# Eight split weight buffers of a decoder trunk, each beginning at its own 64-byte step modulo 512

## The chip, the cores and the metric

The kernel runs as one program on one core of a Trainium2 chip. The time is the device time of one execution in microseconds (us); a lower number is better. Times of the kernel before come from two runs, and the profile from one profiled execution.

## The reference, cut to what matters

The reference computes a decoder trunk of two layers over 512 tokens of width 1024 in float32. Every layer sends the normalised residual stream through one input projection, whose columns feed three groups of heads (latent attention, a pooling mixer and a matrix memory), through one output projection, and through a gated feed-forward part of inner width 2816:

```python
def reference(x, ...):
    h = layer_norm(x, ln0_g, ln0_b)
    for l in range(DEPTH):
        proj = h @ w_in[l]
        cq, ckv, kr, xp, xqk, xv, xo, ipre, fpre = jnp.split(proj, _split_points(), axis=-1)
        a = mla(cq, ckv, kr, g_qn[l], w_uq[l], g_kvn[l], w_ukv[l], cos, sin)
        p = multiscale_pool(xp, w_pool[l], s_pool[l])
        m = mlstm(xqk, xv, xo, ipre, fpre, ...)
        mix = jnp.concatenate([a, p, m], axis=-1) @ w_out[l]
        h = layer_norm(ALPHA * h + mix, ln1_g[l], ln1_b[l])
        f = conv_glu_ffn(h, w_up[l], w_fconv[l], b_fconv[l], w_down[l])
        h = layer_norm(ALPHA * h + f, ln2_g[l], ln2_b[l])
    return h
```

All weight products are dense float32 products; the two largest are `h @ w_up` (1024 by 5632) and `... @ w_down` (2816 by 1024).

## The kernel before, in words

**Split products.** Each float32 operand x is split into hi, which is x cast to the format float32r, and lo = x - hi, cast as well. A product is then three matmuls that add into the same PSUM bank: hi times hi, hi times lo, lo times hi. `mm3` (L159 to L162) does this with the weights as the stationary operand, and `tm_gemm` (L284 to L286) does it with the weights as the moving operand. In a call `T.matmul(o, a, b)` the operand `a` is stationary: a LDWEIGHTS instruction loads its 128 columns, which are 512 bytes in each partition, and there is one LDWEIGHTS for each matmul. The operand `b` is moving and streams through, mostly 512 columns, which are 2048 bytes in each partition. The LDWEIGHTS of a matmul runs while the matmul before it streams.

**Weights.** All weights stand in one list in the order of their use, 93 pieces for each layer and 186 in all, each 128 partitions by up to 1024 floats. `fetch` (L139 to L147) takes the next piece: a DMA from SP's queue into one of two `raw` buffers, the cast into a `hi` buffer on ScalarE (L145), and the subtraction into a `lo` buffer (L146) on VectorE, or on GpSimd for some pieces. There are four hi and four lo buffers, taken in turn, so that piece n reuses the buffers of piece n - 4. `getw` calls `fetch` one piece ahead of the use.

**Stages of a layer.** The input projection is done in pieces `ia` (456 columns at a time), `it` and `ib`; then come the up-projections of attention `uq`, `uk` and `uv`, attention (`s` is scores, `pt` transposed probabilities, `o` values), the output projection (tile name `o` as well, with `hi_o` and `lo_o` as its weights), the feed-forward's up part (`t_up`, 44 pieces for each layer) and its down part (`d`, 22 pieces for each layer). The normalised stream lies transposed in `a_hi` and `a_lo`, the feed-forward's inner activations in `f_hi` and `f_lo`.

**Order.** TensorE's order is written by a small planner (`Order`), which merges instruction streams by fixed costs and due times; the other engines keep program order under a scheduler. Neither reads an address.

**Where the buffers lie.** A tile pool lays its buffers one after the other in SBUF. Each `hi` or `lo` buffer of 1024 floats takes 4096 bytes in a partition, a whole multiple of 512. The start of each buffer in a partition, modulo 512, in the built program:

| buffers | before |
|---|---|
| all four hi and all four lo | 320 |
| a_hi, a_lo (blocks of 512 bytes) | 320 |
| f_hi, f_lo (blocks of 512 bytes) | 128 |
| cq_hi, cq_lo, ck_hi, ck_lo | 0 |
| pt_hi, pt_lo | 0 |
| v (values, four tiles) | 128, 0, 384, 128 |
| qn (queries, four heads) / kn (keys, four heads) | 0, 128, 256, 384 / 256, 256, 384, 256 |

In the up part and in `it` the moving operand is a block of `a_hi` or `a_lo`, and the weights are stationary; in `ia`, `ib` and the output projection it is the other way round. In `d` a weight buffer moves and a block of `f_hi` or `f_lo` is stationary. In `uq` and `uk` the weights are stationary against moving `cq` or `ck`; in `uv` the weights move and `ck` is stationary. In attention `pt` moves against stationary `v`, and `kn` against stationary `qn`.

Of the kernel before, what the change touches and what calls it, by code (L numbers as in the profile page):

```python
# [11 lines left out]
F32R = mybir.dt.float32r  # L12
# [6 lines left out]
P = 128  # L19
# [22 lines left out]
CH = 1024  # L42
# [7 lines left out]


class Order:
    """Merges instruction streams into one order for the tensor engine."""

    def __init__(self):
        self.now = 0.0
# [37 lines left out]
def trunk(ctx: ExitStack, tc: tile.TileContext, I: dict, out: bass.AP, layers=DEPTH):  # L94
# [5 lines left out]
    stream = ctx.enter_context(tc.tile_pool(name="stream", bufs=3))  # L100
# [28 lines left out]
    def bank(name):  # L129
        return psum.tile([P, S], F32, tag="ps", name=name)  # L130

# [1 line left out]
    wlist = []  # L133
    wloaded = []

# [3 lines left out]
    def fetch():  # L139
        src, n, name, eng = wlist[len(wloaded)]  # L140
        raw = stream.tile([P, CH], F32, tag="raw", bufs=2, name="raw_" + name)[:, :n]
        nc.sync.dma_start(raw, src)
        hi = stream.tile([P, CH], F32R, tag="whi", bufs=4, name="hi_" + name)
        lo = stream.tile([P, CH], F32R, tag="wlo", bufs=4, name="lo_" + name)
        A.copy(hi[:, :n], raw)  # L145
        eng.tensor_tensor(lo[:, :n], raw, hi[:, :n].bitcast(F32), ALU.subtract)  # L146
        wloaded.append((hi, lo, name))  # L147
# [3 lines left out]
    def getw(name, ahead=1):  # L151
        while len(wloaded) <= min(used[0] + ahead, len(wlist) - 1):
            fetch()
        hi, lo, nm = wloaded[used[0]]
        assert nm == name, (nm, name)
        used[0] += 1
        return hi, lo
# [206 lines left out]
            for q in range(NF // 2):  # L364
                add_w(I["w_dn"][l, half, q], 1024, f"d{l}_{half}_{q}", V)

# [1 line left out]
    ln0 = ExitStack()  # L368
    lp = ln0.enter_context(tc.tile_pool(name="ln0", bufs=1))
    h = lp.tile([P, NT, D], F32, name="h0")  # L370
# [5 lines left out]
    for i in range(NT):  # L376
        for a in range(0, D, D // 2 if i == 0 else D):
            n = D // 2 if i == 0 else D
            nc.sync.dma_start(h[:, i, a : a + n], I["x"][i * P : (i + 1) * P, a : a + n])
        if i == 0:  # L380
            cols0 = lp.tile([P, 2 * KD], F32, name="cols0")
            nc.sync.dma_start(cols0, I["ln0_c"])
        if i < 3:
            fetch()
        if i == 0:
            nc.sync.dma_start(ident, I["ident"])
# [643 lines left out]
```

## Time and profile before

| | us |
|---|---|
| median of 2 runs (1220.02 to 1220.42) | 1220.22 |
| profiled execution, first to last instruction (its span) | 1215.6 |
| median less span | 4.6 |
| TensorE (PE) busy with matmuls | 1169.8 |
| PE busy with weight loads (PEld) | 954.2 |
| VectorE (DVE) / ScalarE (ACT) / GpSimd (POOL) busy | 640.7 / 474.3 / 282.3 |

The profiled execution's own time is known by its span only; the 4.6 us between the span and the median of the other runs are taken as work around the span that this change doesn't touch. A duration of a matmul in the profile is a modelled one: a matmul's row ends later than the next one starts, so how fast matmuls follow each other is read from the distance of their starts.

### The profile page before, as it was taken

What the parts mean: (1) busy time and instruction counts of PE and PEld (TensorE: products, weight loads), DVE (VectorE), ACT (ScalarE), POOL (GpSimd) and SP (SyncE); (2) the same over time, 40 slices, a digit from 0 to 9 for tenths busy, and PEclk for the clock granted to TensorE, in tenths of its full rate; (3) what the DMA queues carried; (4) which work ended last, traced back from release to release, by engine and by line L of the source; (5) the groups of instructions that cost most, each with busy time, mean ns of one, the idle gap of its engine ahead of it and who ended that gap; (6) DMA issues with size and microseconds to landing.
All of it is one profiled execution on the core that took longest, in us unless ns stands there. A gap on an engine that the chain in (4) does not pass through costs nothing.

```text
span 1215.6 us, 14103 instructions
## 1 busy us (share of the span) xinstructions
PE 1169.8 (96%) x5426; PEld 954.2 (79%) x5426; DVE 640.7 (53%) x929; ACT 474.3 (39%) x815; POOL 282.3 (23%) x240
## 2 busy tenths in 40 slices
PE   5999999989999999999999999997999999999996
PEld 3877878878888888888887787786888888888884
DVE  7775785665434434223388559648544343432325
ACT  4654453525333333211257535525433333331210
POOL 4315610272111111000123264006311111110003
PEclk8999999989999999999999999999999999999998
DMA  5531214123233232323234103041332323322221
GB/s 197 204 118 48 77 53 156 54 102 123 93 98 104 87 104 89 102 87 104 64 137 151 63 31 104 12 180 52 138 101 91 104 88 103 97 94 93 98 70 69
DMA packets 34786, 119.71 MB, mean 98 GB/s; under 512 B 4376, under 2 KB 4888, under 8 KB 34720
## 3 DMA queue, kind: packets, MB, share of 16 engines
q1 hardware_dynamic: 34432, 118.30, 29.2%
q8 instruction: 42, 0.69, 0.2%
q10 hardware_dynamic: 288, 0.52, 0.1%
q14 instruction: 24, 0.20, 0.0%
HBM read 112.50 MB, written 6.31 MB: 98 GB/s over the span
## 4 chain that ended last, share of the span: by engine, by line
PE 77%; DVE 11%; POOL 5%; ACT 3%; issue 2%; DMA 1%; SPq 0%; POOLq 0%; DVEq 0%; ACTq 0%
PE t_up L161 13%; PE t_up L162 13%; PE t_up L160 13%; PE d L286 6%; PE d L284 6%; PE d L285 6%; PE o L284 2%; PE o L285 2%; PE o L286 2%; DVE a_lo L166 1%; POOL ps L521 1%; POOL py L525 1%; PE ib L284 1%; DVE qp L715 1%; PE ib L285 1%
## 5 line engine op out<-in xcount | busy, mean ns | idle before, releaser
L160 PE MATMUL t_up<-a_hi,hi_up 128*128 128x512 f32 (+1 forms) x752 | 284.7, 379 | 9.1 <-ACT a_hi L165 9.1
L161 PE MATMUL t_up<-a_lo,hi_up 128*128 128x512 f32 (+1 forms) x752 | 285.1, 379 | 2.4 <-DVE a_lo L166 2.4
L162 PE MATMUL t_up<-a_hi,lo_up 128*128 128x512 f32 (+1 forms) x752 | 284.1, 378 | 0.0
L146 DVE TENSOR_TENSOR lo_up<-raw_up,hi_up 128x1024 fp32r<-128x1024 f32 x86 | 115.1, 1338 | 172.7 <-ACT hi_up L145 169.2
L160 PEld LDWEIGHTS t_up<-a_hi,hi_up 128*128 128x128 f32 x752 | 143.5, 191 | 34.7 <-ACT a_hi L165 9.5
L145 ACT CAST hi_up<-raw_up 128x1024 fp32r<-128x1024 f32 x88 | 92.8, 1055 | 191.1 <-PE t_up L161 168.0
L161 PEld LDWEIGHTS t_up<-a_lo,hi_up 128*128 128x128 f32 x752 | 143.3, 191 | 29.2 <-DVE a_lo L166 3.1
L905 POOL TENSOR_TENSOR f_lo<-y,f_hi 128x512 fp32r<-128x512 f32 x44 | 77.2, 1753 | 376.1 <-ACT f_hi L904 376.1
L162 PEld LDWEIGHTS t_up<-a_hi,lo_up 128*128 128x128 f32 x752 | 143.5, 191 | 25.7
L146 DVE TENSOR_TENSOR lo_d<-raw_d,hi_d 128x1024 fp32r<-128x1024 f32 x44 | 53.8, 1224 | 165.1 <-ACT hi_d L145 164.7
L284 PE MATMUL d<-hi_d,f_hi 128*128 128x512 f32 x352 | 139.4, 396 | 0.0
L286 PE MATMUL d<-hi_d,f_lo 128*128 128x512 f32 x352 | 139.2, 396 | 0.0
L285 PE MATMUL d<-lo_d,f_hi 128*128 128x512 f32 x352 | 139.2, 395 | 0.0
L145 ACT CAST hi_d<-raw_d 128x1024 fp32r<-128x1024 f32 x44 | 46.3, 1052 | 182.0 <-PE d L286 163.0
L286 PEld LDWEIGHTS d<-hi_d,f_lo 128*128 128x128 f32 x352 | 66.2, 188 | 15.9
L284 PEld LDWEIGHTS d<-hi_d,f_hi 128*128 128x128 f32 x352 | 66.2, 188 | 15.9
L285 PEld LDWEIGHTS d<-lo_d,f_hi 128*128 128x128 f32 x352 | 66.2, 188 | 15.8
L903 DVE TENSOR_TENSOR y<-y,t_up 128x512 f32<-128x512 f32 x44 | 30.2, 687 | 78.1 <-PE t_up L162 74.8
L898 DVE SCALAR_TENSOR_TENSOR y<-t_up,pp,y 128x511 f32<-128x511 f32 x88 | 65.6, 746 | 1.6
L899 ACT ACTIVATE y<-y 128x512 f32<-128x512 f32 x44 | 27.8, 632 | 90.2 <-DVE y L898 90.2
L284 PE MATMUL o<-hi_o,a_hi 128*128 128x512 f32 x128 | 50.9, 398 | 0.0
L286 PE MATMUL o<-hi_o,a_lo 128*128 128x512 f32 x128 | 50.0, 390 | 0.0
(263 smaller groups left out, 1924.0 us busy)
## 6 DMA issues: line engine op xcount, KB each, us to landing
raw_up<-in_w_up_dram SPq DMA_DIRECT2D x88, 512.0 KB, 3.5
raw_d<-in_w_dn_dram SPq DMA_DIRECT2D x44, 512.0 KB, 3.5
raw_o<-in_w_out_dram SPq DMA_DIRECT2D x16, 512.0 KB, 3.5
raw_it<-in_w_it_dram SPq DMA_DIRECT2D x12, 512.0 KB, 3.7
spill<-h SPq DMA_DIRECT2D x8, 512.0 KB, 2.8
raw_ib<-in_w_ib_dram SPq DMA_DIRECT2D x8, 512.0 KB, 3.5
h<-spill SPq DMA_DIRECT2D x8, 512.0 KB, 5.1
raw_ia<-in_w_ia_dram SPq DMA_DIRECT2D x8, 456.0 KB, 4.6
```

Of the source, the lines that this page charges most:

```text
L145: A.copy(hi[:, :n], raw)
L146: eng.tensor_tensor(lo[:, :n], raw, hi[:, :n].bitcast(F32), ALU.subtract)
L160: T.matmul(o, whi, xhi, start=start, stop=False)
L161: T.matmul(o, whi, xlo, start=False, stop=False)
L162: T.matmul(o, wlo, xhi, start=False, stop=stop)
L284: T.matmul(o, xhi, whi, start=at == 0, stop=False)
L285: T.matmul(o, xhi, wlo, start=False, stop=False)
L286: T.matmul(o, xlo, whi, start=False, stop=at == nk - 1)
L898: V.scalar_tensor_tensor(y[:, t:], o[:, : S - t], w(2 - t), y[:, t:], ALU.mult, ALU.add)
L899: A.activation(y, y, AF.Silu)
L903: V.tensor_mul(y, y, o)
L905: G.tensor_sub(fbox["lo"][:, f, :], y, fbox["hi"][:, f, :].bitcast(F32))
```

## The change

The pool that holds the split weights gets eight tags with one buffer each in place of two tags with four buffers each, and each buffer is 16 floats (64 bytes) longer than what is used of it. The buffer for piece n is still the one of piece n - 4. The other lines of the diff take comments away.

```diff
@@ -140,8 +140,9 @@
         src, n, name, eng = wlist[len(wloaded)]
         raw = stream.tile([P, CH], F32, tag="raw", bufs=2, name="raw_" + name)[:, :n]
         nc.sync.dma_start(raw, src)
-        hi = stream.tile([P, CH], F32R, tag="whi", bufs=4, name="hi_" + name)
-        lo = stream.tile([P, CH], F32R, tag="wlo", bufs=4, name="lo_" + name)
+        j = len(wloaded) % 4
+        hi = stream.tile([P, CH + 16], F32R, tag=f"whi{j}", bufs=1, name="hi_" + name)[:, :CH]
+        lo = stream.tile([P, CH + 16], F32R, tag=f"wlo{j}", bufs=1, name="lo_" + name)[:, :CH]
         A.copy(hi[:, :n], raw)
         eng.tensor_tensor(lo[:, :n], raw, hi[:, :n].bitcast(F32), ALU.subtract)
         wloaded.append((hi, lo, name))
```

In the built program every engine has the same instructions in the same order with the same waits as before; only addresses differ. Modulo 512 the weight buffers now start here:

| j | hi | lo |
|---|---|---|
| 0 | 320 | 384 |
| 1 | 448 | 0 |
| 2 | 64 | 128 |
| 3 | 192 | 256 |

The eight buffers together take 512 bytes more in a partition, so every tile that lies behind them moves by exactly 512 bytes and keeps its place modulo 512: `a_hi` and `a_lo` 320, `f_hi` and `f_lo` 128, `cq`, `ck` and `pt` 0. The two `raw` buffers lie ahead of them and do not move.

## The prediction

> **What bounds the kernel now.** I read the page first: the busy times, the slices and the chain that ended last.
>
> ```profile
> span 1215.6 us, 14103 instructions
> ...
> PE 1169.8 (96%) x5426; PEld 954.2 (79%) x5426; DVE 640.7 (53%) x929; ACT 474.3 (39%) x815; POOL 282.3 (23%) x240
> ...
> PEclk8999999989999999999999999999999999999998
> ...
> PE 77%; DVE 11%; POOL 5%; ACT 3%; issue 2%; DMA 1%; SPq 0%; POOLq 0%; DVEq 0%; ACTq 0%
> ```
>
> TensorE has work in 96% of the span at the full granted clock, and three quarters of the chain are its matmuls. So the time is set by how closely matmuls follow each other, and next I read the groups of instructions with shapes kept apart, for their counts and durations:
>
> ```profile
> L161 PE MATMUL t_up<-a_lo,hi_up 128*128 128x512 f32 x656 | 255.2, 389 | 0.0
> L285 PE MATMUL d<-lo_d,f_hi 128*128 128x512 f32 x352 | 139.2, 395 | 0.0
> L285 PE MATMUL o<-lo_o,a_hi 128*128 128x512 f32 x128 | 49.9, 390 | 0.0
> L161 PE MATMUL t_it<-a_lo,hi_it 128*128 128x512 f32 x96 | 37.9, 395 | 0.0
> L161 PE MATMUL t_up<-a_lo,hi_up 128*128 128x256 f32 x96 | 29.9, 311 | 2.4 <-DVE a_lo L166 2.4
> L285 PE MATMUL ia<-lo_ia,a_hi 128*128 128x456 f32 x64 | 25.2, 394 | 0.1
> L285 PE MATMUL ib<-lo_ib,a_hi 128*128 128x512 f32 x64 | 24.9, 390 | 0.0
> L161 PE MATMUL uq<-cq_lo,hi_uq 128*128 128x512 f32 x36 | 14.2, 396 | 0.0
> L161 PE MATMUL uk<-ck_lo,hi_uk 128*128 128x512 f32 x16 | 6.3, 395 | 0.0
> L285 PE MATMUL uv<-lo_uv,ck_hi 128*128 128x512 f32 x16 | 6.3, 391 | 0.0
> ```
>
> Each row is one of the three matmuls of a split product, so a stage has three times its count. What matters is that 512 columns do not cost the same everywhere: 389 to 390 ns in `t_up`, `ib` and the output projection, 395 to 396 in `d`, `uq` and `uk`. (`t_it` has 395 as well, but part of it runs early and between waits.) The timeline gives the same difference in the distance of starts, first for `t_up` in mid-stage, then for `d`:
>
> ```profile
> 349.77 0.39 PE L160 MATMUL t_up<-a_hi,hi_up 128*128 128x512 f32 x1
> ...
> 351.13 0.39 PE L160 MATMUL t_up<-a_hi,hi_up 128*128 128x512 f32 x1
> ```
>
> ```profile
> 599.81 0.40 PE L284 MATMUL d<-hi_d,f_hi 128*128 128x512 f32 x1
> ...
> 602.14 0.40 PE L285 MATMUL d<-lo_d,f_hi 128*128 128x512 f32 x1
> ```
>
> There are six matmuls from the first to the last row of `t_up`, 1.36 us / 6 = 226.7 ns each, and ten in `d`, 2.33 / 10 = 233.0 ns. The instructions are of one shape and PE waits for nothing in either place. The tables of starts offer a reason: in `t_up` the moving block and the weights being loaded both start at 320 modulo 512, while in `d` the moving weights start at 320 and the loaded block of `f` at 128. The output projection moves weights too, as `d` does, but with equal steps, and its 390 is near `t_up`. So I looked for other pairs of starts in the timeline. In `uv` (the first three rows) and `uq`, then in attention's values and in the scores of head 0 and head 1:
>
> ```profile
> 745.11 0.39 PE L284 MATMUL uv<-hi_uv,ck_hi 128*128 128x512 f32 x1
> ...
> 745.80 0.39 PE L160 MATMUL uq<-cq_hi,hi_uq 128*128 128x512 f32 x1
> ...
> 746.50 0.40 PE L160 MATMUL uq<-cq_hi,hi_uq 128*128 128x512 f32 x1
> ```
>
> ```profile
> 179.89 0.39 PE L160 MATMUL o<-pt_hi,v 128*128 128x512 f32 x1
> ...
> 180.59 0.34 PE L160 MATMUL o<-pt_hi,v 128*128 128x384 f32 x1
> ```
>
> ```profile
> 161.00 0.39 PE L161 MATMUL s<-kn,qn 128*128 128x512 f32 x1
> ...
> 161.46 0.40 PE L773 MATMUL s<-kp,qp 128*128 128x512 f32 x1
> ```
>
> ```profile
> 167.23 0.39 PE L161 MATMUL s<-kn,qn 128*128 128x512 f32 x1
> ...
> 167.69 0.40 PE L773 MATMUL s<-kp,qp 128*128 128x512 f32 x1
> ```
>
> I call the start of the loaded operand less that of the moving one, modulo 512, the distance. `t_up` has 0. The other spacings, and what each costs above 226.7: `uv`, distance 192, 0.69 / 3 = 230.0, +3.3 ns; `uq`, distance 320, 0.70 / 3 = 233.3, +6.6; `d`, also 320, 233.0, +6.3; attention's values, distance 128, 0.70 / 3 = 233.3, +6.6; head 0's scores, distance 256, 0.46 / 2 = 230.0, +3.3; head 1's, distance 384, 0.46 / 2 = 230.0, +3.3. Two stages that share nothing but the distance 320 agree, and none that I found in steady 512-column work is under `t_up`. That is the base of the forecast. The weak points: rows have steps of 10 ns, so the last two, over two matmuls, are good to about 5 ns, and each distance stands for one pair of tiles.
>
> The Trainium skill ("SBUF — State Buffer", section "Who interferes with whom") says that TensorE has two independent read ports, one for the moving operand and one for LDWEIGHTS, and waits on nobody. By that rule no distance could cost anything, and the sum would be zero; the rows above do not fit it without another reason for the 6 ns. I keep it as a rival.
>
> **The change part by part.**
>
> *Tags and rotation.* A piece still waits for the piece four before it, so no wait, DMA or instruction is added or moved: 0. The fetch chain has room too:
>
> ```profile
> DVE lo_up L146 <- ACT hi_up L145: 169.2, 48, 7.9
> ACT hi_up L145 <- PE t_up L161: 168.0, 71, 5.4
> ...
> ACT hi_d L145 <- PE d L286: 163.0, 36, 4.5
> ```
>
> ```profile
> L145 ACT CAST hi_up<-raw_up 128x1024 fp32r<-128x1024 f32 x88 | 92.8, 1055 | 191.1 <-PE t_up L161 168.0 <-DMA raw_up<-in_w_up_dram 14.4 <-PE o L286 8.7
> ```
>
> The cast waits for TensorE to give a buffer back, not the reverse, and 168.0 + 163.0 us of such waiting over the 88 + 44 pieces is 2.5 us of room for each. If the new starts made the cast a tenth slower, the room would hide it; without that room a tenth of its 1055 ns on 132 pieces would be 14 us.
>
> *Weights against `a`.* These have distance 0 in all cases now: `t_up` 3 x 656 = 1968 matmuls of 512 columns, output projection 3 x 128 = 384, `it` 3 x 96 = 288, `ib` 3 x 64 = 192; 2832 in all. Afterwards, with `a` at 320, the distances are: hi buffers 0, 128, 256, 384; lo buffers 64, 192, 320, 448 (in `ib` and the output projection the same set with the sign turned). The hi buffer is used in two of three matmuls. For 128, 192, 256, 320 and 384 I take the prices above: 6.6, 3.3, 3.3, 6.6, 3.3. For 64 and 448 the trace has nothing; I bound them by 3.3 and 6.6 and take the middle, 5. Hi: (0 + 6.6 + 3.3 + 3.3) / 4 = 3.3 ns. Lo: (5 + 3.3 + 6.6 + 5) / 4 = 5.0 ns. Weighted (2 x 3.3 + 5.0) / 3 = 3.9 ns, times 2832 = +11.0 us. PE is the bound throughout these stages, so this lands on the end one for one; in `it` and `ib` some may vanish in waits, at most 480 x 3.9 = 1.9 us.
>
> *The narrower ones.* The 288 matmuls of `t_up` with 256 columns and 192 of `ia` with 456 belong here as well. At 3.9 ns they would add 1.9 us, but both stand at the layers' waits for the norm (the row above shows such a wait on `a_lo`); I take 0 and leave 1.9 to the range.
>
> *`d`.* 3 x 352 = 1056 matmuls, all at distance 320 now, 6.5 ns above. Afterwards, with `f` at 128: hi 320, 192, 64, 448, that is (6.6 + 3.3 + 5 + 5) / 4 = 5.0; lo 256, 128, 0, 384, that is (3.3 + 6.6 + 0 + 3.3) / 4 = 3.3. Weighted 4.4 ns, a gain of 2.1 x 1056 = -2.2 us.
>
> *`uq`, `uk`.* 3 x 36 + 3 x 16 = 156 matmuls at distance 320, afterwards spread alike: -2.1 x 156 = -0.3 us. `uv` (48 matmuls) stays near its 3.3: 0.
>
> Sum: 11.0 - 2.2 - 0.3 = +8.5 us on the span of 1215.6. With the 4.6 us between span and median that stay, 1220.2 + 8.5 is about 1228.5; I say 1228, since the coarse rows of the scores rather overstate.
>
> Bounds of this case: if every distance but 0 costs 3.3 ns, five sixths of the 2832 pay, 2360 x 3.3 = +7.8, and `d` with the 156 gains (6.5 - 3.0) x 1212 = -4.2, so +3.6 us, 1224. If every one costs 6.6, 2360 x 6.6 = +15.6 and `d` gains 0.5 x 1212 = 0.6, with 1.9 for the narrow ones +16.9, 1237.
>
> **The rivals.**
>
> *The steps do nothing.* The 6 ns may belong to the tiles themselves, for instance how far apart the two operands lie (`a` is next to the weights, `f`, `cq`, `pt` and `v` are not), which a shift of under 512 bytes keeps. For it: in `t_up` and the output projection the fast pairs are also the close ones. Against it: `uv` and `uq` both pair weights with a far tile and differ by 3.3 ns. The time stays at 1220. It is also what the skill's rule on the two ports gives; that sentence changes no number here.
>
> *Spreading takes collisions away, and it is faster.* Equal steps could be the worst case that one thinks of: both streams begin in the same step at the same moment. The nearest row for a matmul without any such collision is the bfloat16 warm-up, three matmuls of 512 columns at the end of its run:
>
> ```profile
> 5.78 0.81 PE L375 MATMUL wp<-wz 128*128 128x512 bf16 x3
> ```
>
> With 0.38 us for the last one, two spacings take 0.43 us, 215 ns each: `t_up` is 12 ns above this. If half of that went for the 2360 matmuls whose distance becomes unequal, 2360 x 6 = 14 us, and if `d` came to the same 221 ns in eleven of twelve, 12 x 968 = 12 us: 1194. If only a fifth of it went from the 2360, 2360 x 2.4 = 6 us: 1214. It decides as soon as an unequal distance has a spacing under 226.7 ns. Against it: no row of 512 columns of an unequal distance shows that; all are above.
>
> *Neighbouring steps are bad.* Distances 64 and 448 are in no row. In the new layout they fall on two of four lo buffers against `a`, 2832 / 6 = 472 matmuls, and on two of four hi buffers in `d`, 1056 / 3 = 352. For 2% (24.4 us) in all, these 824 would have to pay (24.4 - 8.5) / 824 = 19 ns more than the 5 assumed, a spacing above 250 ns. The largest mean in any row of 512 columns that I read is 233. At that price it would be 1245.
>
> **How the numbers follow.** My forecast has a chance of 0.62, no effect 0.20, faster by spreading 0.12 (half of it by more than 2%), bad neighbours 0.06. The predicted time is the forecast's, 1228. The range goes from 1217 to 1237: it holds the forecast's bounds, the case of no effect, and the small end of the faster one; what is left out is most of the faster rival and the bad neighbours. A measurement of this kernel is taken to tell 2% from no change. Faster by over 2%: 0.06; slower by over 2%: 0.06; within 2%: 0.88.
>
> **What would show it.** In the changed kernel the rows of `t_up` must show a mean above 389, about 393, and the timeline must show spacings that change from piece to piece with a period of four: 226.7 with the hi buffer at 320, larger with the others. `d` must fall from 395 to about 393, with one lo buffer in four (at 128, where `f` is) at 226 to 227. The waits of `hi_up` for TensorE stay near 168 us or grow. If `t_up` stays at 389 in all pieces, the steps do nothing and the 6 ns have another cause; if any buffer shows under 226 ns, spreading helps; if two lo buffers in `t_up` stand out by 20 ns, it is the neighbours. The forecast's size fails where distances 128 and 256 have other prices than in attention.

## The result, and the profile after

The changed kernel takes 1231.5 us (1231.13 to 1231.87) against 1220.22 us before: a ratio of 1.0095 with a 95% interval of 1.0066 to 1.0124. It is 11 us slower; 1228 was forecast, with a range of 1217 to 1237.

The page and the groups by shape of the changed kernel, in the columns of before (the diff makes line numbers one higher):

```profile
span 1229.3 us, 14103 instructions
...
PE 1182.0 (96%) x5426; PEld 955.5 (78%) x5426; DVE 640.2 (52%) x929; ACT 473.8 (39%) x815; POOL 282.1 (23%) x240
```

```profile
L163 PE MATMUL t_up<-a_hi,lo_up 128*128 128x512 f32 x656 | 259.4, 395 | 0.0
...
L162 PE MATMUL t_up<-a_lo,hi_up 128*128 128x512 f32 x656 | 257.5, 393 | 0.0
...
L285 PE MATMUL d<-hi_d,f_hi 128*128 128x512 f32 x352 | 139.5, 396 | 0.0
L287 PE MATMUL d<-hi_d,f_lo 128*128 128x512 f32 x352 | 138.6, 394 | 0.0
L286 PE MATMUL d<-lo_d,f_hi 128*128 128x512 f32 x352 | 138.5, 394 | 0.0
...
L286 PE MATMUL o<-lo_o,a_hi 128*128 128x512 f32 x128 | 50.3, 393 | 0.0
```

VectorE, ScalarE and GpSimd are as busy as before within 0.6 us; PE has 12.2 us more for the same instructions. In `t_up` a matmul takes 393 to 395 ns in place of 389, in this row of the output projection 393 in place of 390, in `d` 394 to 396 in place of 395 to 396. What ScalarE waited for stays long, so no buffer became late:

```profile
ACT hi_up L146 <- PE t_up L162: 179.8, 72, 5.4
...
ACT hi_d L146 <- PE d L287: 162.3, 36, 4.6
```

The timeline of `t_up` shows the buffers. Each row is the first matmul of a piece of 24; the pieces use, in this order, hi and lo at 320 and 384, 448 and 0, 64 and 128, 192 and 256:

```profile
344.30 0.39 PE L161 MATMUL t_up<-a_hi,hi_up 128*128 128x512 f32 x1
...
349.83 0.39 PE L161 MATMUL t_up<-a_hi,hi_up 128*128 128x512 f32 x1
...
355.41 0.39 PE L161 MATMUL t_up<-a_hi,hi_up 128*128 128x512 f32 x1
...
360.95 0.39 PE L161 MATMUL t_up<-a_hi,hi_up 128*128 128x512 f32 x1
...
366.52 0.39 PE L161 MATMUL t_up<-a_hi,hi_up 128*128 128x512 f32 x1
```

That is 230.4, 232.5, 230.8 and 232.1 ns for each matmul (5.53, 5.58, 5.54 and 5.57 us over 24), against 226.7 before. Every piece is slower, and pieces with buffers 256 bytes apart (the first and third, the second and fourth) are alike. The mean is 231.5, +4.8 ns. So the first piece isn't the fast one that the forecast wanted, though its hi buffer lies at 320 as `a` does.

### The profile page after: what moved, and what is told of

The parts are those of the page before. It is cut to its first block, busy times and chain, and to the rows that moved or that the text cites. A ratio compares the mean times of both kernels' runs of the same rounds, so it can differ in the third digit from the quotient of the medians.

```text
span 1229.3 us, 14103 instructions
## 1 busy us (share of the span) xinstructions
PE 1182.0 (96%) x5426; PEld 955.5 (78%) x5426; DVE 640.2 (52%) x929; ACT 473.8 (39%) x815; POOL 282.1 (23%) x240
## 4 chain that ended last, share of the span: by engine, by line
PE 82%; DVE 10%; ACT 3%; DMA 2%; issue 1%; POOL 1%; SPq 0%; DVEq 0%; POOLq 0%; ACTq 0%
PE t_up L162 13%; PE t_up L163 13%; PE t_up L161 13%; PE d L285 6%; PE d L287 6%; PE d L286 6%; PE o L287 2%; PE o L285 2%; PE o L286 2%; DVE a_lo L167 1%; PE num L650 1%; PE t_it L161 1%; PE t_it L163 1%; PE t_it L162 1%; DVE qp L716 1%
## 5 line engine op out<-in xcount | busy, mean ns | idle before, releaser
L163 PE MATMUL t_up<-a_hi,lo_up 128*128 128x512 f32 (+1 forms) x752 | 288.5, 384 | 0.0
L146 ACT CAST hi_up<-raw_up 128x1024 fp32r<-128x1024 f32 x88 | 92.6, 1053 | 201.1 <-PE t_up L162 179.8
L285 PE MATMUL d<-hi_d,f_hi 128*128 128x512 f32 x352 | 139.5, 396 | 0.0
L287 PE MATMUL d<-hi_d,f_lo 128*128 128x512 f32 x352 | 138.6, 394 | 0.0
L286 PE MATMUL d<-lo_d,f_hi 128*128 128x512 f32 x352 | 138.5, 394 | 0.0
L146 ACT CAST hi_d<-raw_d 128x1024 fp32r<-128x1024 f32 x44 | 46.2, 1049 | 182.3 <-PE d L287 162.3
```

The costliest lines, as they stand in the source:

```text
L163: T.matmul(o, wlo, xhi, start=False, stop=stop)
L285: T.matmul(o, xhi, whi, start=at == 0, stop=False)
L286: T.matmul(o, xhi, wlo, start=False, stop=False)
L287: T.matmul(o, xlo, whi, start=False, stop=at == nk - 1)
```

## The experiments

Two theories stood against each other. **A, the distance:** a matmul pays by the distance, modulo some length, between the start of its moving operand and the start of the weights loaded meanwhile; that is the forecast's. **B, the change:** it costs when the starts differ from one load or moving operand to the next, as hi and lo do in the changed kernel. No experiment leaves any work out.

### One start for each piece

```diff
-        hi = stream.tile([P, CH], F32R, tag="whi", bufs=4, name="hi_" + name)
-        lo = stream.tile([P, CH], F32R, tag="wlo", bufs=4, name="lo_" + name)
+        j = len(wloaded) % 4
+        hi = stream.tile([P, CH], F32R, tag=f"whi{j}", bufs=1, name="hi_" + name)
+        lo = stream.tile([P, CH + (16 if j < 3 else 80)], F32R, tag=f"wlo{j}", bufs=1, name="lo_" + name)[:, :CH]
```

> hi and lo of one piece begin at the same step, and the pieces take turns: 320, 384, 448, 0 modulo 512 (a at 320, f at 128 stay). So the weights' start is constant within a piece, and one run gives the spacing at four constant distances. Theory A (each matmul pays by the distance between its moving operand and the weights loaded meanwhile): in t_up the pieces show about 227, 233 (if a distance of 64 is like one of 320), 233 and 230 ns, mean 230.8; d shows 233, 230, 230 and 233. In all 2832 x 4.1 - 1056 x 1.8 = about +10 us, 1230. Theory B (a change of start from one load to the next is what costs, as hi and lo alternate in the changed kernel): within a piece nothing changes, so nearly all pieces of t_up stay at 227, and the time stays within 3 us of 1220.

Measured: 1226.22 us, ratio 1.0057 (1.0043 to 1.0071). The timeline of this kernel, first matmuls of pieces at 320, 384, 448 and 0 in `t_up`, then of pieces at 0, 320, 384 and 448 in `d`:

```profile
343.61 0.39 PE L161 MATMUL t_up<-a_hi,hi_up 128*128 128x512 f32 x1
...
349.06 0.40 PE L161 MATMUL t_up<-a_hi,hi_up 128*128 128x512 f32 x1
...
354.66 0.39 PE L161 MATMUL t_up<-a_hi,hi_up 128*128 128x512 f32 x1
...
360.23 0.39 PE L161 MATMUL t_up<-a_hi,hi_up 128*128 128x512 f32 x1
...
365.75 0.39 PE L161 MATMUL t_up<-a_hi,hi_up 128*128 128x512 f32 x1
```

```profile
515.21 0.40 PE L285 MATMUL d<-hi_d,f_hi 128*128 128x512 f32 x1
...
520.79 0.40 PE L285 MATMUL d<-hi_d,f_hi 128*128 128x512 f32 x1
...
526.40 0.39 PE L285 MATMUL d<-hi_d,f_hi 128*128 128x512 f32 x1
...
531.86 0.40 PE L285 MATMUL d<-hi_d,f_hi 128*128 128x512 f32 x1
...
537.37 0.40 PE L285 MATMUL d<-hi_d,f_hi 128*128 128x512 f32 x1
```

| distance (loaded less moving), modulo 256 | `t_up`, ns | `d`, ns |
|---|---|---|
| 0 | 227.1 | 227.5 |
| 64 | 233.3 | 233.8 |
| 128 | 232.1 | 232.5 |
| 192 | 230.0 | 229.6 |

In `t_up` the loaded operand was moved, in `d` the moving one, and they pair the weights with different tiles; yet both give the same four numbers once the distance is taken modulo 256. So with starts that stay constant theory A holds, and B alone is refuted. (A's time of 1230 was too high: with the prices of the table its own sum is 2832 x 3.9 - 1056 x 2.5 = +8.4, 1228. The 2 us that are left weren't followed.) The distance is what counts, not the place of the tiles: 64 bytes move the same tile from 227 to 233 ns.

### Hi at one start, lo 64 bytes further

```diff
         hi = stream.tile([P, CH], F32R, tag="whi", bufs=4, name="hi_" + name)
+        if not wloaded:
+            stream.tile([P, 16], F32, tag="pad1", bufs=1, name="pad1")
         lo = stream.tile([P, CH], F32R, tag="wlo", bufs=4, name="lo_" + name)
+        if not wloaded:
+            stream.tile([P, 112], F32, tag="pad2", bufs=1, name="pad2")
```

> All four hi buffers begin at 320 and all four lo buffers at 384; every piece is alike. In the changed kernel the pieces with this pair of starts show 228, 229 and 236 ns in turn in t_up. Theory A: the two matmuls that load hi have distance 0 and 227 ns, the one that loads lo has 64 and 233; mean 229, time 1220 + 2832 x 2.2 less about 1 us in d = 1225. Theory B: the change between hi and lo costs whatever the distances are; as in the changed kernel 228, 229, 236, mean 231, with the long one while hi loads; 2832 x 4.3 = +12 us less about 1 in d, 1231.

Measured: 1232.93 us, 1.0113 (1.0097 to 1.0128), as slow as the changed kernel with only two starts. Its groups by shape:

```profile
L166 PE MATMUL t_up<-a_hi,lo_up 128*128 128x512 f32 x656 | 260.7, 397 | 0.0
L165 PE MATMUL t_up<-a_lo,hi_up 128*128 128x512 f32 x656 | 257.2, 392 | 0.0
L164 PE MATMUL t_up<-a_hi,hi_up 128*128 128x512 f32 x656 | 255.2, 389 | 0.0
L289 PE MATMUL d<-lo_d,f_hi 128*128 128x512 f32 x352 | 140.3, 399 | 0.0
```

By distance alone L165 should be long, since lo is loaded while it runs; instead it is the one after, with 397. The size is read from the starts, here of two matmuls of `t_up` with 96 from the first to the second:

```profile
343.55 0.39 PE L164 MATMUL t_up<-a_hi,hi_up 128*128 128x512 f32 x1
...
365.74 0.39 PE L164 MATMUL t_up<-a_hi,hi_up 128*128 128x512 f32 x1
```

That is 22.19 us / 96 = 231.1 ns, 4.4 above 226.7, where the distances alone would give 6.6 / 3 = 2.2. And `d`, with one row at 399, takes 0.8 us more in its three rows together than before, although its distances (64 for hi, 0 for lo) became better. So a change of start within the three matmuls costs on top of the distances. Theory B's number, 1231, is the nearer one.

### Lo 256 bytes from hi

The same edit with two pads of 64 floats.

> All hi buffers begin at 320, all lo buffers at 64 modulo 512, which is 256 apart. In the changed kernel buffers that are 256 apart show the same spacings, so both theories say that starts count modulo 256 only: t_up stays at 227 in all three matmuls, time 1220. If they count modulo 512, theory A with 3.3 ns for a distance of 256 gives 2832 / 3 x 3.3 = +3 us, 1223, and theory B, with a change at every pass from hi to lo, about +12 us, 1232.

Measured: 1220.05 us, 1.0002 (0.9993 to 1.0011): nothing, where 64 bytes gave 13 us. No rows of this run are read here; the last experiment below repeats the step and shows its rows.

### All eight weight buffers 64 bytes further

The same edit with a pad of 16 floats ahead of hi and one of 112 behind lo, none between.

> All eight weight buffers begin at the same step as before the change, but 64 bytes further, 384 in place of 320. No start changes from piece to piece or from hi to lo. By the prices at constant distances t_up, it, ib and the output projection go to distance 64 and d to distance 0 modulo 256: 2832 x 6.6 - 1056 x 6.6 = +11.7 us, 1231, with 233.3 ns in t_up and 226.7 in d, the two changing places. If what costs is only that starts differ among the buffers, nothing changes: 1220.

Measured: 1228.62 us, 1.0074 (1.0061 to 1.0088). Groups of this kernel:

```profile
L165 PE MATMUL t_up<-a_lo,hi_up 128*128 128x512 f32 x656 | 259.5, 396 | 0.0
...
L289 PE MATMUL d<-lo_d,f_hi 128*128 128x512 f32 x352 | 137.0, 389 | 0.0
L288 PE MATMUL o<-hi_o,a_hi 128*128 128x512 f32 x128 | 51.3, 401 | 0.0
L290 PE MATMUL o<-hi_o,a_lo 128*128 128x512 f32 x128 | 50.3, 393 | 0.0
L289 PE MATMUL o<-lo_o,a_hi 128*128 128x512 f32 x128 | 49.8, 389 | 0.0
```

`t_up` and `d` change places, 389 to 396 and 395 to 389, with all eight starts equal. So it isn't that the buffers' starts coincide or not among themselves, but how they stand to the other operand. The 1231 expected was too high because I gave `ib` and the output projection a distance of 64; there the weights move, and the distance is 320 - 384, which is 192 modulo 256. With 3.3 ns in place of 6.6 for these 576 matmuls the sum is 1.9 us less, 1229. The three rows of the output projection rise from 398, 390 and 390 to 401, 393 and 389, by 1.7 ns on the mean.

### Steps of 32 bytes

As with one start for each piece, with 8 floats in place of 16 and 104 in place of 80.

> As in the run with four starts by piece, but the pieces begin at 320, 352, 384 and 416, steps of 32 bytes. Prices at constant starts so far, by distance modulo 256: 0 ns at 0, 6.6 at 64, 5.7 at 128, 2.7 at 192. If the price follows the distance in bytes, 32 bytes cost between 0 and 6.6 in t_up, near 230 ns, and 96 about 233; total about 2832 x 4.0 - 1056 x 3.8 = +7, 1227. If only whole 64-byte steps count, 32 shows the 226.7 of distance 0 and 96 the 233.3 of 64, and the total is 2832 x 3.3 - 1056 x 3 = +6, 1226. The spacings tell these apart, the time doesn't.

Measured: 1232.41 us, 1.0104 (1.0084 to 1.0124). First matmuls of pieces at 320, 352, 384 and 416 in `t_up`:

```profile
346.80 0.40 PE L161 MATMUL t_up<-a_hi,hi_up 128*128 128x512 f32 x1
...
352.28 0.39 PE L161 MATMUL t_up<-a_hi,hi_up 128*128 128x512 f32 x1
...
357.87 0.40 PE L161 MATMUL t_up<-a_hi,hi_up 128*128 128x512 f32 x1
...
363.47 0.39 PE L161 MATMUL t_up<-a_hi,hi_up 128*128 128x512 f32 x1
...
369.08 0.40 PE L161 MATMUL t_up<-a_hi,hi_up 128*128 128x512 f32 x1
```

228.3, 232.9, 233.3 and 233.8 ns. A distance of 32 bytes costs nearly all that 64 do; neither half of the expectation was right about it, and the time is 5 to 6 us above both of its numbers. In `d` the piece at 416 has a distance of 128 - 416, which is 224 modulo 256:

```profile
519.41 0.40 PE L285 MATMUL d<-hi_d,f_hi 128*128 128x512 f32 x1
...
525.01 0.39 PE L285 MATMUL d<-hi_d,f_hi 128*128 128x512 f32 x1
```

5.60 us / 24 = 233.3 ns, so 32 bytes to the other side cost as much. Three of the four distances of `d` thus stay at 233, and the gain that the expectation put there (3 to 4 us) is mostly missing.

### Only a_lo moved

```diff
     a_hi = pers.tile([P, NT, KD, P], F32R, name="a_hi")
+    pers.tile([P, 16], F32, name="a_pad")
     a_lo = pers.tile([P, NT, KD, P], F32R, name="a_lo")
+    pers.tile([P, 112], F32, name="a_pad2")
```

> The kernel before with a_lo alone moved by 64 bytes, to 384; the weights stay at 320. In t_up one of three matmuls then moves from another step than its neighbours, while all loads stay at one step. By distance alone (192 modulo 256 for that one, 2.7 ns), t_up rises by 0.9 ns to 227.6; in ib and the output projection one of three loads has distance 64, 2.2 ns on the mean; 2256 x 0.9 + 576 x 2.2 = +3.3 us, 1223. If a change of step within the three matmuls costs on top, as with hi and lo apart (231.1 where distances alone give 228.9), t_up comes to about 229.8, and the time to 1228 or more.

Measured: 1230.96 us, 1.0095 (1.0081 to 1.0109). Groups of this kernel:

```profile
L164 PE MATMUL t_up<-a_hi,lo_up 128*128 128x512 f32 x656 | 258.6, 394 | 0.0
L163 PE MATMUL t_up<-a_lo,hi_up 128*128 128x512 f32 x656 | 258.3, 394 | 0.0
...
L287 PE MATMUL d<-lo_d,f_hi 128*128 128x512 f32 x352 | 139.2, 396 | 0.0
```

All weights lie where they were, one moving operand of three lies 64 bytes off, and `t_up` is at 394. Two starts in `t_up`, again with 96 matmuls from the first to the second:

```profile
344.20 0.39 PE L162 MATMUL t_up<-a_hi,hi_up 128*128 128x512 f32 x1
...
366.47 0.40 PE L162 MATMUL t_up<-a_hi,hi_up 128*128 128x512 f32 x1
```

That is 22.27 us / 96 = 232.0 ns, 5.3 above 226.7, where the distances alone give 3.3 / 3 = 1.1. Here the change of start within the three matmuls is the larger part. This kernel, with the weights untouched, loses what the changed kernel loses.

### f moved to the weights' start, and cq and ck too

```diff
+            fa.tile([P, 48], F32, name="f_pad")
             fbox["hi"] = fa.tile([P, NF, S], F32R, name="f_hi")
```

> The kernel before with f_hi and f_lo moved by 192 bytes, so that they begin at 320 modulo 512, where the weights and a begin too. Theory A and B: d goes from 233.3 to the 226.7 ns of t_up, 1056 x 6.6 = -7.0 us, 1213. If the spacing of d belongs to its tiles (f lies far from the weights) and not to the steps, d stays at 233 and the time at 1220.

Measured: 1212.51 us, 0.9945 (0.9932 to 0.9957). Then with `mix.tile([P, 16], F32, name="c_pad")` ahead of `cq_hi` in addition:

> f at 320 as in the run with f moved, and cq and ck moved by 64 bytes as well, so that uq, uk and uv have distance 0 modulo 256. By the prices, 156 x 6.6 + 48 x 2.7 = 1.2 us below that run's 1212.5, 1211.3; uq falls from 233 to 227. If the steps did nothing in these short stages, 1212.5. The probabilities pt move with them, and attention's values change from distances 128, 0, 128, 128 to 64, 192, 64, 64, under 0.2 us.

Measured: 1212.12 us, 0.9939 (0.9926 to 0.9951). Groups of the second kernel:

```profile
L161 PE MATMUL t_up<-a_lo,hi_up 128*128 128x512 f32 x656 | 255.2, 389 | 0.0
...
L285 PE MATMUL d<-lo_d,f_hi 128*128 128x512 f32 x352 | 137.0, 389 | 0.0
...
L161 PE MATMUL uq<-cq_lo,hi_uq 128*128 128x512 f32 x36 | 14.0, 389 | 0.0
```

`d` fell to 389 by the first edit and `uq` from 396 to 389 by the second; the 1 us of the second is too little to be told in the time. Both beat the kernel before and the changed one.

### The same with lo 256 bytes from hi

> The kernel with f, cq and ck moved (1212.1 us), and in addition all lo buffers moved by 256 bytes, from 320 to 64 modulo 512; hi stays at 320. If starts count modulo 256, t_up and d stay at 226.7 ns in all three matmuls and the time at 1212. If they count modulo 512, a step within the three matmuls changes, as with hi and lo 64 bytes apart, and t_up comes to 229 to 231 ns, the time to 1219 or more.

The edits of the last kernel and of the one with 256 bytes, together. Measured: 1210.87 us, 0.9931 (0.9914 to 0.9949). Groups of this kernel:

```profile
L164 PE MATMUL t_up<-a_hi,hi_up 128*128 128x512 f32 x656 | 255.2, 389 | 0.0
L165 PE MATMUL t_up<-a_lo,hi_up 128*128 128x512 f32 x656 | 255.2, 389 | 0.0
L166 PE MATMUL t_up<-a_hi,lo_up 128*128 128x512 f32 x656 | 255.2, 389 | 0.0
L288 PE MATMUL d<-hi_d,f_hi 128*128 128x512 f32 x352 | 137.1, 389 | 0.0
```

All three matmuls stay at 389, so starts count modulo 256 and a change by 256 is none.

## Why the prediction was right, and where it wasn't

**The base held.** PE was the bound, the spacing of matmuls differs with the starts of their operands, and the kernel before had the best case, distance 0, in its largest stages. The run with all eight buffers moved together shows that with nothing else changed. It also refutes the rival that the steps do nothing: the rule of two independent read ports (the Trainium skill, "SBUF — State Buffer", section "Who interferes with whom") doesn't describe this; 64 bytes of shift cost 7 ns of 227 for each matmul.

**The prices were partly wrong.** The forecast worked modulo 512 and had 6.6, 3.3, 3.3, 6.6 and 3.3 ns for 128, 192, 256, 320 and 384. The first piece run gives, above 226.7, 0.4 at distance 0, 6.6 at 64, 5.4 at 128 and 3.3 at 192, and the same again 256 further. So 256 was given 3.3 too much (the scores' rows over two matmuls were too coarse) and 384 2.1 too little. With these prices the forecast's own sum for the weights against `a` is (2 x (0.4 + 5.4) / 2 + (6.6 + 3.3) / 2) / 3 = 3.6 ns, not far from its 3.9: the errors nearly cancel, and that is luck.

**The mechanism lacked a part.** Measured was +4.8 in `t_up`, so some 1.2 ns remain: the price of the change of start from hi to lo and back, which the forecast didn't have. In `t_up` that is 1968 x (4.8 - 3.9) = 1.8 us of the miss. The first piece shows it best: 230.4 ns, where the forecast had 226.7 for the two loads of hi and about 232 for lo, 228.4 on the mean. So of the signs that the prediction named the mean of `t_up` came (393 to 395), but not the pattern: no piece is at 226.7, the period is two and not four, and in `d` the matmul that moves the lo buffer at 128 takes 235 to 236 ns, not 226 to 227.

**`d` gained less.** Forecast was -2.2 us; the rows give 139.5 + 138.6 + 138.5 against 139.4 + 139.2 + 139.2, that is -1.2. The weights' starts there change between hi and lo as well.

**The rest of the miss.** The 1.8 us of `t_up` and the 1.0 us of `d` come to 2.8, as much as the measured +11.3 is above the forecast's sum of +8.5. The 4.6 us around the span were mis-sized: the changed kernel's profiled execution took 1231.13 us with a span of 1229.3, so only 1.8 us lie around it, and 1.7 to 1.9 us do so in every execution for which both are on record. So the profiled execution of before must have been some 2.8 us under its median. The forecast was added to the median and isn't moved by this. Against the medians the change is +11.3, against the two spans +13.7; PE's busy time, +12.2, lies between. How the 2.4 us between the medians and the spans, and the share of the input projection, split up wasn't followed.

**The rivals.** Faster by spreading: of the 512-column stages read here none has a mean under 389, the 226.7 of before. Single spacings in the changed kernel do lie under it, but beside longer ones: in `d`, with lo at 0, the three matmuls of a product take 234.3, 225.8 and 234.2 ns, so 231.4 on the mean. With 256 columns unequal distances are faster (last section), on 288 matmuls, too few to turn the result. Bad neighbours: 64 costs more than 128 and 192, but it is at 233, not 250. The cover of the cast and the subtraction held, with 179.8 and 162.3 us of waiting.

What stays open is why a change of start costs: that it does is shown by three kernels, but no run shows what the two streams do inside. Which of the three matmuls pays isn't settled either. With lo 64 bytes off it is the one after the load of lo (397), and in the output projection with `a_lo` moved it is the one after the load of `a_lo` (397, with 392 for the one before it); but in the pieces of the changed kernel with hi at 448 the first of the three is the longest (233.9, 231.2 and 232.0 ns). Where starts stay constant, the weights that a matmul uses and those that are loaded beside it start alike, so those runs can't tell by which of the two it pays.

## What to carry to other kernels

Where TensorE is the bound with long float32r matmuls, look at the starts of the moving and the stationary operand: with 512 columns, lay all of them at the same place modulo 256, in all tiles that meet, and take the time of matmuls from the distance of starts stage by stage, since a stage that is a few per cent slower with the same shapes is worth a reason. Spreading buffers over different starts was the wrong way here; moving the two tiles of `f` by 192 bytes gained 0.55%.

## What the runs showed of the hardware that I had not expected

A 512-column float32r matmul with a weight load beside it took 226.7 ns where moving and loaded operand start at the same place modulo 256, 232.9 at 32 bytes, 233.3 at 64, 233.8 at 96, 232.1 at 128, 230.0 at 192 and 233.3 at 224, and the sign counts, since 64 and 192 differ. With starts that stay constant, the same distance costs the same whether the moving or the loaded operand is shifted. When the start of one of three operands in turn is 64 bytes off, a matmul takes 2.2 ns (weights) or 4.2 ns (moving) more on the mean than the distances give.

With 256 columns it goes the other way. The half-wide part of `t_up`, at a granted clock of 1.00, in the kernel before (54 matmuls from the first to the last row) and in the one with all weight buffers 64 bytes further (49 matmuls):

```profile
258.28 0.28 PE L160 MATMUL t_up<-a_hi,hi_up 128*128 128x256 f32 x1
...
264.62 0.28 PE L162 MATMUL t_up<-a_hi,lo_up 128*128 128x256 f32 x1
```

```profile
262.18 0.28 PE L166 MATMUL t_up<-a_hi,lo_up 128*128 128x256 f32 x1
...
267.63 0.28 PE L166 MATMUL t_up<-a_hi,lo_up 128*128 128x256 f32 x1
```

Distance 0 has 6.34 / 53 = 119.6 ns, distance 64 has 5.45 / 48 = 113.5. So which of the two is better depends on the width, and the figures above hold for 512 columns alone.
